# Narrower dst one-hots, group by group, in a sorted gather–transform–scatter on one core

## The chip, the core and the metric

The kernel runs on one core of a Trainium2 chip. The metric is the time of one execution on the device in microseconds (us), and the median of several executions counts. In this text PE is TensorE, DVE VectorE, ACT ScalarE, POOL GpSimd and SP SyncE.

## What is computed

There are 4096 nodes with 256 features and 262144 edges. Every edge takes the features of its source node, multiplies them by `w_msg`, and adds the result to the row of its destination node; every node also gets its own features times `w_self`.

```
self_out = nodes @ w_self
msg = nodes[edges_src] @ w_msg
np.add.at(agg, edges_dst, msg)
return self_out + agg
```

The inputs are drawn with a fixed seed, so the edges are the same in every execution.

## The kernel before

The kernel never gathers rows. It counts how many edges lead from a source to a destination and multiplies the counts by Y = nodes @ w_msg.

**Sort (first 153 us).** Each edge becomes one number, its key. In the key stand the segment of 373 destinations, the block of 128 sources, the destination inside the segment and the source inside the block. A sorting network of min and max operations on DVE (lines 854 to 1080) puts the keys nearly in order; PE and ACT turn columns and, beside that, compute Y. SP queues the loads of the edges, then the store of the nodes in bf16 and 64 transposing loads of XT (lines 211 to 280). POOL fills constants and then issues the loads of the weights and nodes (lines 218 to 272).

**Count (153 to 418 us).** The sorted edges form 2048 chunks of 128. A chunk's smallest key gives its base, and its edges lie within W = 96 steps of destination above it. For groups of chunks (`sizes`, line 466: 37 groups, most of them 64 chunks) DVE writes one-hots (`onehots`, line 471): `e_oh`, 128 columns for the source, and `d_oh`, W columns for the destination. They come in pieces of 16 columns, so a group of 64 chunks has eight pieces of `e_oh` and six of `d_oh`, each of 1024 elements a partition; two buffers of each exist, so DVE is at most two groups ahead. For every chunk PE loads `e_oh` as weights and streams the W columns of `d_oh` (`count_mm`, lines 534 and 741) into one of six PSUM banks at a place that a register gives (`poff`). A bank holds the counts of one run: 374 columns of one segment and source block, and W more as spill into the next run. There are 352 runs. The first chunks of a run meet empty columns, so `clear` (line 547) first streams zeros over two strips of GAP = 84 columns; GAP is also the largest step between two bases that is allowed.

**Apply.** When a run is complete, ACT casts its bank to SBUF (`evac`, line 556, 470 columns), and PE multiplies it with Y in three matmuls of 256 columns (`apply_run`, line 617). The spill of the run before is added either by a fourth matmul (line 623, for early runs and the last four) or by DVE (`merge`, line 577), which joins consecutive runs into one add when all of them are there. After each of 11 segments ACT copies the output rows (line 634) and POOL adds them to the output in DRAM.

**Order.** The code is written out in order of issue; nothing is rescheduled. While PE works on one group, DVE writes the one-hots of the next in four pieces of code, and the merges stand between them (line 719). The second half of the chunks gets its last sort steps during the count phase (`late_work`, line 423). `next_bases`, `misplaced` and `total` (lines 659 to 687) test that every chunk kept to its limits; if one did not, a slow general path follows (line 774).

Of the kernel before, what the change touches and what calls it, by code (L numbers as in the profile page):

```python
# [9 lines left out]
P = 128  # L10
# [110 lines left out]
def kernel(  # L121
# [230 lines left out]
    def bases(h, own):  # L352
        z = slice(h * GP, (h + 1) * GP)
        sort.note(
            nc.vector.tensor_reduce(out=k16[:, z], in_=_view3(own, P), axis=AX.X, op=ALU.min), SIZE
        )
        sort.note(muladd(k16i[:, z], k16[:, z], 1, D6 * P), GP)
        sort.note(tss(out=g7[:, z], in_=k16i[:, z], scalar=-P, op=ALU.bitwise_and), GP)
        sort.note(muladd(g7f[:, z], g7[:, z], 1 if h else -1, TOP - D6 * P if h else D6 * P), GP)

# [104 lines left out]

    sizes = [8, 24, 32, 40, 48] + [NC] * 12 + [56, 48] + [NC] * 15 + [32, 16, 16]
    assert sum(sizes) == NCOL and sum(sizes[:19]) == SIZE
    late = list(late_work())
    due = sum(cost for cost, _ in late)

    def onehots(c, n, res):
        if c in split_at:
            split_vals(c, split_at[c])
# [13 lines left out]
        for w, (nm, wid, row) in enumerate((("e", P, jrow), ("d", W, drow))):  # L487
            o = ohp.tile([P, NC // 2, wid, 2], BF16, name=nm + "_oh", tag=nm, bufs=2)
            if n <= 16:
                shp = [P, n // 2, wid, 2]  # L490
                tt(
                    out=o[:, 0:n // 2], in0=pair[:, g, w].unsqueeze(2).to_broadcast(shp),
                    in1=row[:].unsqueeze(1).to_broadcast(shp), op=ALU.is_equal,
                )
            else:
                for j in range(0, wid, NW):
# [50 lines left out]
    def clear(r):  # L547
        b = (r % RING) * BW
        after = [evac_of[r - RING]] if r >= RING else []
        zone = bass.AP(  # L550
            tensor=ring.tensor, offset=ring[:, b:b + 1].offset,
            ap=[list(ring[:].ap[0]), [SW + W - GAP, 2], [1, GAP]],
        )
        count_mm(zone, zer[:, 0, :], zer[:, 1:3, 0:GAP], True, after)

    def evac(r):
        at = ats[r % NAT]
        b = (r % RING) * BW
        ins = nc.scalar.copy(out=at[:, 0:SW + W], in_=ring[:, b:b + SW + W]).ins  # L559
        tc.declare_no_dep(  # L560
            ins, group="count", keep=[last_mm[0]], reason="disjoint banks by static schedule"
        )
        tc.add_manual_dep(ins, last_mm[0].name, DEP, reason="run complete")
        tc.add_to_no_dep_group("evac", ins)
        evac_of[r] = ins
        at_of[r] = at
# [10 lines left out]
    def merge(upto):  # L577

        upto = min(upto, NRUN - TAIL - 1)
        while merged[0] < upto:  # L580
# [20 lines left out]
    def apply_run(r):  # L601
# [14 lines left out]
        for t in range(NT):  # L616
# [54 lines left out]
    def misplaced():  # L671
# [19 lines left out]
    if True:  # L691
# [11 lines left out]
        for c in range(NCOL):  # L703
# [26 lines left out]
            if c % NREG == 0:  # L730
# [380 lines left out]
```

## Time and profile before

| what | us |
|---|---|
| median of 3 executions (426.31 to 427.47) | 426.39 |
| the profiled execution | 428.29 |
| span of its trace | 426.5 |

A trace lists for each engine when an instruction began and how long it took. Matmuls overlap in the pipeline, so their cost is the distance from one start to the next, not the duration that is printed; the same holds, to a smaller degree, on DVE. A line of the timeline joins instructions of one kind that follow each other ("x5"), with the start of the first and the time to the end of the last.

### The profile page before, as it was taken

The numbers are of one execution on the slowest core, as the hardware profiler recorded it, in microseconds if no ns is written. First come the engines' busy times: TensorE is split into PE (matmuls) and PEld (weight loads), VectorE is DVE, ScalarE is ACT, GpSimd is POOL, SyncE is SP. The second block draws the span as 40 slices with busy tenths as digits, with TensorE's granted clock in tenths as the row PEclk, the third lists the DMA queues.
The fourth block names the chain that finished last, engine by engine and source line by source line (L and its number), as shares of the span: only waits on it lengthen the run. The fifth ranks groups of instructions, "written<-read, shape, count | busy, mean of one in ns | idle before, by whom it ended". The sixth has DMA issues, their size and how long they took to land.

```text
span 426.5 us, 10578 instructions
## 1 busy us (share of the span) xinstructions
PE 339.9 (80%) x4085; PEld 288.7 (68%) x4094; DVE 383.8 (90%) x892; ACT 254.1 (60%) x515; POOL 39.1 (9%) x59
## 2 busy tenths in 40 slices
PE   0004950878787689999989899899999999999994
PEld 0001530455555357999988898798989988989993
DVE  7999999999999989999999979679999999999750
ACT  3200220155468047877777779697877877877771
POOL 5300000000000000002010030111101020102010
PEclk9999995899999899999999999699999999999999
DMA  8796111111119200003021030221203030303031
GB/s 314 141 159 197 28 24 27 25 27 25 25 32 308 79 0 2 2 2 39 0 26 16 2 37 5 55 33 15 27 2 38 6 33 4 38 2 37 4 37 38
DMA packets 31600, 20.38 MB, mean 48 GB/s; under 512 B 13244, under 2 KB 30397, under 8 KB 31549
## 3 DMA queue, kind: packets, MB, share of 16 engines
q0 software_dynamic: 8976, 6.18, 12.5%
q1 hardware_dynamic: 21876, 11.53, 9.1%
q10 hardware_dynamic: 697, 1.98, 1.2%
q8 instruction: 33, 0.54, 0.5%
q14 instruction: 18, 0.15, 0.1%
HBM read 8.92 MB, written 10.76 MB: 46 GB/s over the span
## 4 chain that ended last, share of the span: by engine, by line
PE 50%; DVE 38%; ACT 6%; issue 3%; DMA 2%; SPq 0%; DVEq 0%; ACTq 0%
PE out_ps L617 20%; PE ring L535 20%; DVE XA L866 18%; DVE XS L866 6%; DVE e_oh L511 5%; DVE d_oh L511 4%; PE out_ps L623 3%; PE tp_sw L992 3%; ACT atr L559 2%; PE warm L886 2%; DMA d<-in_edges_dst_dram 2%; DVE off L478 2%; DVE atr L589 1%; PE out_ps L745 1%; ACT XA L996 1%
## 5 line engine op out<-in xcount | busy, mean ns | idle before, releaser
L559 ACT CAST atr<-ring 128x470 bf16<-128x470 f32 x352 | 180.0, 556 | 58.4 <-PE ring L535 53.2
L617 PE MATMUL out_ps<-Y,atr 128*128 128x256 bf16 x1056 | 169.0, 274 | 3.3 <-ACT o_sb L635 2.7
L535 PE MATMUL ring<-d_oh,e_oh 128*128 128x96 bf16 x2048 | 154.5, 207 | 3.0 <-DVE d_oh L511 1.9
L535 PEld LDWEIGHTS <-e_oh 128*128 128x128 bf16 x2048 | 136.5, 98 | 9.0 <-issue 2.3
L617 PEld LDWEIGHTS <-atr 128*128 128x128 bf16 x1056 | 95.9, 98 | 9.9 <-issue 2.8
L866 DVE TENSOR_TENSOR XA<-XA 128x512 f32<-128x512 f32 (+32 forms) x142 | 92.8, 702 | 3.7 <-ACT XA L996 2.0
L511 DVE TENSOR_SCALAR e_oh<-off 128x1024 bf16<-128x1024 int16 (+5 forms) x254 | 87.1, 404 | 9.2 <-PE ring L535 6.2
L535 PE MATMUL ring<-zer 128*128 128x168 bf16 x352 | 82.9, 235 | 3.9 <-ACT atr L559 3.8
L886 PE MATMUL warm<-zw 128*128 128x512 bf16 x97 | 32.0, 442 | 56.1 <-DVE XA L866 51.2
L511 DVE TENSOR_SCALAR d_oh<-off 128x1024 bf16<-128x1024 int16 (+5 forms) x204 | 69.1, 402 | 0.0
L758 POOL DMA_DIRECT2D out_dram<-o_sb x30 | 30.2, 1007 | 363.1 <-ACT atr L559 363.1
L996 ACT COPY XA<-tp_sw 128x512 f32<-128x512 f32 x24 | 14.2, 592 | 77.8 <-PE tp_sw L992 77.8
L886 PEld LDWEIGHTS <-zw 128*128 128x128 bf16 x105 | 10.5, 107 | 73.8 <-issue 45.7
L478 DVE TENSOR_TENSOR off<-pair,rows 128x2048 int16<-128x2048 int16 (+5 forms) x34 | 38.8, 1140 | 1.2
L535 PEld LDWEIGHTS <-zer 128*128 128x128 bf16 x352 | 34.1, 97 | 8.3 <-ACT atr L559 5.6
L623 PE MATMUL out_ps<-Y,atr 128*96 128x256 bf16 x118 | 32.1, 272 | 0.0
L589 DVE TENSOR_TENSOR atr<-atr 128x288 bf16<-128x288 bf16 (+3 forms) x84 | 23.0, 293 | 8.9 <-ACT atr L559 8.7
L992 PE MATMUL tp_sw<-XA,id 128*128 128x128 f32 x192 | 24.3, 278 | 6.1 <-DVE XA L866 6.0
L992 PEld LDWEIGHTS tp_sw<-XA,id 128*128 128x128 f32 x192 | 22.4, 190 | 9.5 <-DVE XA L866 3.6
L287 PE MATMUL y_ps<-wcat,XT 128*128 128x256 bf16 x128 | 20.8, 270 | 7.4 <-ACT Y L291 3.3
L866 DVE TENSOR_TENSOR XS<-XS 128x512 f32<-128x512 f32 (+16 forms) x40 | 24.1, 653 | 0.5
L866 DVE TENSOR_TENSOR XR<-XR 128x1004 f32<-128x1004 f32 (+13 forms) x28 | 23.1, 868 | 0.2
(107 smaller groups left out, 175.9 us busy)
## 6 DMA issues: line engine op xcount, KB each, us to landing
out_dram<-o_sb POOLq DMA_DIRECT2D x20, 128.0 KB, 3.4
nodes_bf<-in_nodes_dram POOLq DMA_DIRECT2D x1, 2048.0 KB, 16.7
nodes_bf_dram<-nodes_bf SPq DMA_DIRECT2D x1, 2048.0 KB, 8.7
out_dram<-nodes_bf SPq DMA_DIRECT2D x4, 512.0 KB, 5.1
out_dram<-XA SPq DMA_DIRECT2D x4, 512.0 KB, 2.9
out_dram<-o_sb POOLq DMA_DIRECT2D x10, 117.0 KB, 3.1
s<-in_edges_src_dram ACTq DMA_DIRECT2D x2, 512.0 KB, 5.1
d<-in_edges_dst_dram SPq DMA_DIRECT2D x2, 512.0 KB, 6.0
```

Source lines behind the costliest of these rows:

```text
L287: nc.tensor.matmul(out=y_ps[:], lhsT=XT[:, k, t * P:(t + 1) * P], rhs=wcat[:, k0 + k, :], start=(k == 0), stop=(k == 1),)
L478: tt(out=v[:, 0:n // 2].rearrange("p g w (k i) -> p (g w) k i", i=2), in0=pair[:, g].rearrange("p g w i -> p (g w) i").unsqueeze(2).to_bro ...
L511: ins = tss(out=o[:, 0:n // 2, j:j + m].rearrange("p g k i -> p g (k i)"), in_=v[:, 0:n // 2, w, 0:2 * m], scalar=float((0 if w else ON_AC ...
L535: mm = nc.tensor.matmul(out=ap, lhsT=lhsT, rhs=rhs, start=start, stop=True, skip_group_check=True,).ins
L559: ins = nc.scalar.copy(out=at[:, 0:SW + W], in_=ring[:, b:b + SW + W]).ins
L589: tt(out=atr[:, j:j + n, 0:W], in0=atr[:, j:j + n, 0:W], in1=atr[:, i:i + n, SW:SW + W], op=ALU.add,)
L617: nc.tensor.matmul(out=out_ps[:, t, :], lhsT=at[:, t * P:(t + 1) * P], rhs=Y[:, b, :], start=(b == 0 and not last and t % 2 == 0), stop=(b ...
L623: nc.tensor.matmul(out=out_ps[0:W, 0, :], lhsT=spill[:, SW:SW + W], rhs=Y[:, b, :], start=False, stop=False, skip_group_check=True,)
L758: nc.gpsimd.dma_start(out=dst, in_=src, accum_op=ALU.add).ins,
L866: self.nc.vector.tensor_tensor(out=out, in0=in0, in1=in1, op=op),
L886: self.nc.tensor.matmul(out=w[:], lhsT=self.zw[:, 0:P], rhs=self.zw[:], start=True, stop=True).ins
L992: self.nc.tensor.matmul(out=tp[:, g * P:(g + 1) * P], lhsT=self.turned(rots[8 * h + 4 * t + g]), rhs=sel(x)[:, 4 * t + g], start=True, sto ...
```

## The change

Each group of chunks now has, in a table, its own width of `d_oh` and its own largest step (`GROUPS`: chunks, width, step). The widths are 80 to 95, on average 90.3 per chunk. Everything that followed W or GAP follows the table: the last of the six pieces of `d_oh` is cut to width − 80 columns, the count matmul streams only the width, the clear streams two strips of step plus the difference of the widths that a run meets, the cast takes 374 columns plus the widest spill, and a merge takes only runs of equal spill together. The destination values are shifted so that a narrower one-hot uses the last columns of the same row of constants. The shift and the step test need a value per chunk, so POOL writes a small table with 111 memsets, and two more DMAs of SP bring it to all partitions (`by_q`).

```diff
+GROUPS = [
+    (8, 80, 73), (24, 89, 73), (32, 90, 77), (40, 92, 77), (48, 92, 79), (64, 91, 82),
+    (64, 90, 81), (64, 89, 81), (64, 88, 78), (64, 93, 82), (64, 92, 79), (64, 88, 82),
+    (64, 94, 79), (64, 92, 79), (64, 90, 78), (64, 93, 77), (64, 92, 80), (56, 90, 83),
+    (48, 85, 77), (64, 88, 75), (64, 90, 80), (64, 95, 78), (64, 91, 80), (64, 87, 80),
+    (64, 89, 79), (64, 87, 83), (64, 87, 80), (64, 90, 79), (64, 91, 81), (64, 90, 77),
+    (64, 91, 79), (64, 90, 81), (64, 89, 82), (64, 95, 82), (32, 94, 79), (16, 91, 81),
+    (16, 88, 75),
+]
...
+    c = 0
+    for n, wid, gap in GROUPS:
+        z = slice(c // GP, (c + n) // GP)
+        shift = (W - wid) * P
+        for i, v in enumerate((gap, D6 * P + shift, TOP - D6 * P - shift)):
+            nc.gpsimd.memset(brow_c[:, i, z], float(v))
+        c += n
+    nc.sync.dma_start(tab_d[:, :], brow_c[:].rearrange("o t m -> o (t m)"))
+    nc.sync.dma_start(
+        by_q[:], tab_d.rearrange("o (t h q) -> q (o t) h", t=3, h=PARTS)
+    )
...
+    def about(r):
+        c0, c1 = max(0, clear_at(r) - 1), min(NCOL - 1, evac_at(r) + 1)
+        z = GROUPS[group_of[c0]:group_of[c1] + 1]
+        return max(w for _, w, _ in z), min(w for _, w, _ in z), max(g for _, _, g in z)
...
-                        in_=v[:, 0:n // 2, w, 0:2 * m], scalar=float((0 if w else ON_ACT) - j),
+                        in_=v[:, 0:n // 2, w, 0:2 * m], scalar=float((-j0 if w else ON_ACT) - j),
...
-        count_mm(zone, zer[:, 0, :], zer[:, 1:3, 0:GAP], True, after)
+        count_mm(zone, zer[:, 0, :], zer[:, 1:3, 0:n], True, after)
...
-        ins = nc.scalar.copy(out=at[:, 0:SW + W], in_=ring[:, b:b + SW + W]).ins
+        n = SW + spill_of(r)
+        ins = nc.scalar.copy(out=at[:, 0:n], in_=ring[:, b:b + n]).ins
...
+            m = spill_of(d - 1)
+            while (
+                n < min(upto - d + 1, NAT - i, NAT - j) and not by_pe(d + n)
+                and spill_of(d + n - 1) == m
+            ):
                 n += 1
...
-        stt(out=bad[:], in0=v[:], scalar=float(GAP), in1=bad[:], op0=ALU.is_gt, op1=ALU.add)
+        tt(
+            out=v[:].rearrange("p (h k) -> p h k", h=PARTS),
+            in0=v[:].rearrange("p (h k) -> p h k", h=PARTS),
+            in1=by_q[:, 0, :].unsqueeze(2).to_broadcast([P, PARTS, GP]), op=ALU.is_gt,
+        )
+        tt(out=bad[:], in0=bad[:], in1=v[:], op=ALU.add)
...
             count_mm(
-                ring[:, bass.ds(off, W)], e[:, ci // 2, :, ci % 2], d[:, ci // 2, :, ci % 2], False
+                ring[:, bass.ds(off, wid)], e[:, ci // 2, :, ci % 2], d[:, ci // 2, 0:wid, ci % 2],
+                False,
             )
```

On DVE, the second half of the count phase: the one-hots of chunks 1408 to 1471, from the middle of `e_oh` on. `atr` is the row of casted runs that a merge adds to; 32x32 is 32 pairs of chunks by 16 columns of two. Before:

```order
L511 TENSOR_SCALAR e_oh<-off 128x32x32 x5
L589 TENSOR_TENSOR atr<-atr 128x3x96
L511 TENSOR_SCALAR e_oh<-off 128x32x32 x2
L511 TENSOR_SCALAR d_oh<-off 128x32x32 x3
L589 TENSOR_TENSOR atr<-atr 128x4x96
L511 TENSOR_SCALAR d_oh<-off 128x32x32 x3
```

The same place after the change, with a width of 87:

```order
L552 TENSOR_SCALAR e_oh<-off 128x32x32 x5
L637 TENSOR_TENSOR atr<-atr 128x2x87
L637 TENSOR_TENSOR atr<-atr 128x89
L552 TENSOR_SCALAR e_oh<-off 128x32x32 x2
L552 TENSOR_SCALAR d_oh<-off 128x32x32 x3
L637 TENSOR_TENSOR atr<-atr 128x4x89
L552 TENSOR_SCALAR d_oh<-off 128x32x32 x2
L552 TENSOR_SCALAR d_oh<-off 128x32x14
```

The last piece shrinks to rows of 14 elements, and the merge of three runs becomes one of two and one of one, because the spills are 87 and 89 wide.

On POOL, at the program's start, where the constants end and the DMAs of the weights and nodes begin. Before:

```order
L264 COPY rows<-jrow 128x32
L265 COPY rows<-drow 128x32
L268 DMA wcat<-in_w_self_dram 128x2x256
L270 DMA wcat<-in_w_msg_dram 128x2x256
L272 DMA nodes_bf<-in_nodes_dram 128x32x256
```

After, from the 61st of the 111 memsets on:

```order
L283 MEMSET brow_c 1x8 x45
L283 MEMSET brow_c 1x4 x3
L283 MEMSET brow_c 1x2 x6
L290 DMA wcat<-in_w_self_dram 128x2x256
L292 DMA wcat<-in_w_msg_dram 128x2x256
L294 DMA nodes_bf<-in_nodes_dram 128x32x256
```

All memsets stand ahead of the three DMAs. On SP, two DMAs are put ahead of the store of the nodes and the 64 transposes. After the change:

```order
L222 DMA s_4_143<-in_edges_src_dram 128x224
L277 DMA kd<-ones_sent 1x1
L285 DMA tab_d<-brow_c 1x768
L286 DMA by_q<-tab_d 128x6x1
L295 DMA nodes_bf_dram<-nodes_bf 128x32x256
L298 DMA_TRANSPOSE XT<-nodes_bf_dram 128x128 x64
```

## Rows read from the trace of the kernel before

**Rows 1.** Page: busy time by engine, granted clock in 40 slices

```profile
PE 339.9 (80%) x4085; PEld 288.7 (68%) x4094; DVE 383.8 (90%) x892; ACT 254.1 (60%) x515; POOL 39.1 (9%) x59
...
PEclk9999995899999899999999999699999999999999
```

**Rows 2.** Windows of the count phase: length, busy us by engine, PEclk, DMA

```profile
153.70:256.00 102.30, 97.45 (x1333) 89.22 (x1335) 96.54 (x236) 77.20 (x143) 8.79 (x9) 1.00 0.11 13
256.00:277.00 21.00, 18.48 (x229) 16.07 (x227) 16.29 (x52) 16.22 (x35) 1.17 (x2) 0.84 0.14 30
277.00:297.00 20.00, 19.30 (x281) 17.67 (x278) 17.60 (x52) 17.68 (x35) 3.53 (x3) 1.00 0.16 20
297.00:338.00 41.00, 40.40 (x606) 38.01 (x604) 39.66 (x108) 33.41 (x68) 4.72 (x5) 1.00 0.18 21
338.00:384.00 46.00, 44.58 (x658) 41.46 (x657) 44.85 (x129) 35.56 (x72) 7.09 (x7) 1.00 0.17 19
384.00:418.00 34.00, 33.84 (x489) 31.63 (x486) 24.04 (x68) 25.34 (x50) 4.89 (x6) 1.00 0.21 25
```

**Rows 3.** Timeline of PE: start, us to the end of the last, what

```profile
310.23 0.23 PE L535 MATMUL ring<-zer 128*128 128x168 bf16 x1
310.30 0.38 PE L535 MATMUL ring<-d_oh,e_oh 128*128 128x96 bf16 x5
310.52 0.81 PE L617 MATMUL out_ps<-Y,atr 128*128 128x256 bf16 x6
```

**Rows 4.** Timeline of DVE over one group of 64 chunks

```profile
310.60 1.23 DVE L478 TENSOR_TENSOR off<-pair,rows 128x2048 int16<-128x2048 int16 x1
...
312.55 1.76 DVE L511 TENSOR_SCALAR e_oh<-off 128x1024 bf16<-128x1024 int16 x5
314.22 0.35 DVE L589 TENSOR_TENSOR atr<-atr 128x384 bf16<-128x384 bf16 x1
314.49 0.76 DVE L511 TENSOR_SCALAR e_oh<-off 128x1024 bf16<-128x1024 int16 x2
...
316.17 0.45 DVE L589 TENSOR_TENSOR atr<-atr 128x96 bf16<-128x96 bf16 x3
316.52 1.10 DVE L511 TENSOR_SCALAR d_oh<-off 128x1024 bf16<-128x1024 int16 x3
317.66 1.23 DVE L478 TENSOR_TENSOR off<-pair,rows 128x2048 int16<-128x2048 int16 x1
```

**Rows 5.** Groups by shape on DVE: busy us, mean ns, idle before

```profile
L511 DVE TENSOR_SCALAR d_oh<-off 128x1024 bf16<-128x1024 int16 x162 | 58.3, 423 | 0.0
...
L511 DVE TENSOR_SCALAR d_oh<-off 128x512 bf16<-128x512 int16 x12 | 2.7, 289 | 0.0
...
L461 DVE TENSOR_SCALAR pair<-vals_r 128x512 int16<-128x512 int16 x2 | 1.2, 603 | 0.0
```

**Rows 6.** Where one-hots end and PE begins on them: PE's timeline

```profile
296.77 0.21 PE L535 MATMUL ring<-d_oh,e_oh 128*128 128x96 bf16 x1 [0.67 <-DVE d_oh L511]
...
355.71 0.25 PE L535 MATMUL ring<-d_oh,e_oh 128*128 128x96 bf16 x2
```

**Rows 7.** Chain of waits in order of time: start, us, what

```profile
269.25 1.44 PE out_ps L617 x6
...
278.62 0.66 PE out_ps L617 x6
...
354.59 1.02 DVE d_oh L511 x3
```

**Rows 8.** Timeline of POOL at the start

```profile
3.50 0.09 POOL L257 MEMSET top<- 128x1 f32 x1
3.54 0.09 POOL L258 MEMSET limit<- 128x1 f32 x1
...
14.37 0.88 POOL L268 DMA_DIRECT2D wcat<-in_w_self_dram  x1 [7.87 <-ACT XS L232]
```

**Rows 9.** Timeline of PE at the end of the sort

```profile
141.77 4.44 PE L886 MATMUL warm<-zw 128*128 128x512 bf16 x11 [3.44 <-DVE XS L866]
```

More of the change, by code (lines that the diff above doesn't have):

```diff
@@ L147 @@
     kd = dram.tile([1, NCOL + 1], FP32, name="kd")
+    tab_d = dram.tile([1, 3 * NCOL // (NCOL // PARTS // P)], FP32, name="tab_d")
     order = tc.manual_schedule()
@@ L247 @@
     ones_sent = const.tile([1, 1], FP32, name="ones_sent")
+    brow_c = const.tile([1, 3, NCOL // GP], FP32, name="brow_c")
+    by_q = const.tile([P, 3, PARTS], FP32, name="by_q")
     jrow = const.tile([P, P, 2], I16, name="jrow")
@@ L358, in bases @@
         sort.note(tss(out=g7[:, z], in_=k16i[:, z], scalar=-P, op=ALU.bitwise_and), GP)
-        sort.note(muladd(g7f[:, z], g7[:, z], 1 if h else -1, TOP - D6 * P if h else D6 * P), GP)
+        sort.note(
+            stt(
+                out=g7f[:, z], in0=g7[:, z], scalar=1.0 if h else -1.0,
+                in1=by_q[:, 1 + h, h:h + 1].to_broadcast([P, GP]), op0=ALU.mult, op1=ALU.add,
+            ), GP
+        )
     def offsets(h):
@@ L464, with spill_of @@
     split_at = {0: 32, 32: 152, 152: 600, 600: SIZE, SIZE: SIZE + 512, SIZE + 512: NCOL}
-    sizes = [8, 24, 32, 40, 48] + [NC] * 12 + [56, 48] + [NC] * 15 + [32, 16, 16]
-    assert sum(sizes) == NCOL and sum(sizes[:19]) == SIZE
+    sizes = [n for n, _, _ in GROUPS]
+    assert sum(sizes) == NCOL
     late = list(late_work())
     due = sum(cost for cost, _ in late)
+    group_of = [g for g, n in enumerate(sizes) for _ in range(n)]
+    def about(r):
+        c0, c1 = max(0, clear_at(r) - 1), min(NCOL - 1, evac_at(r) + 1)
+        z = GROUPS[group_of[c0]:group_of[c1] + 1]
+        return max(w for _, w, _ in z), min(w for _, w, _ in z), max(g for _, _, g in z)
+    def spill_of(r):
+        return about(r)[0]
     def onehots(c, n, res):
+        width = GROUPS[group_of[c]][1]
         if c in split_at:
@@ L488, in onehots @@
             o = ohp.tile([P, NC // 2, wid, 2], BF16, name=nm + "_oh", tag=nm, bufs=2)
+            j0 = (0, W - width)[w]
+            wid -= j0
             if n <= 16:
@@ L491, in onehots @@
                 tt(
-                    out=o[:, 0:n // 2], in0=pair[:, g, w].unsqueeze(2).to_broadcast(shp),
-                    in1=row[:].unsqueeze(1).to_broadcast(shp), op=ALU.is_equal,
+                    out=o[:, 0:n // 2, 0:wid],
+                    in0=pair[:, g, w].unsqueeze(2).to_broadcast(shp),
+                    in1=row[:, j0:].unsqueeze(1).to_broadcast(shp), op=ALU.is_equal,
                 )
@@ L549, in clear @@
         after = [evac_of[r - RING]] if r >= RING else []
+        most, least, gap = about(r)
+        n = gap + most - least
         zone = bass.AP(
             tensor=ring.tensor, offset=ring[:, b:b + 1].offset,
-            ap=[list(ring[:].ap[0]), [SW + W - GAP, 2], [1, GAP]],
+            ap=[list(ring[:].ap[0]), [SW + most - n, 2], [1, n]],
         )
-        count_mm(zone, zer[:, 0, :], zer[:, 1:3, 0:GAP], True, after)
+        count_mm(zone, zer[:, 0, :], zer[:, 1:3, 0:n], True, after)
     def evac(r):
@@ L586, in merge @@
             n = 1
-            while n < min(upto - d + 1, NAT - i, NAT - j) and not by_pe(d + n):
+            m = spill_of(d - 1)
[3 more added lines that the diff above has]
+            ):
                 n += 1
             tt(
-                out=atr[:, j:j + n, 0:W], in0=atr[:, j:j + n, 0:W],
-                in1=atr[:, i:i + n, SW:SW + W], op=ALU.add,
+                out=atr[:, j:j + n, 0:m], in0=atr[:, j:j + n, 0:m],
+                in1=atr[:, i:i + n, SW:SW + m], op=ALU.add,
             )
@@ L622, in apply_run @@
             if t == 0 and r > 0 and by_pe(r):
+                m = spill_of(r - 1)
                 nc.tensor.matmul(
-                    out=out_ps[0:W, 0, :], lhsT=spill[:, SW:SW + W], rhs=Y[:, b, :],
+                    out=out_ps[0:m, 0, :], lhsT=spill[:, SW:SW + m], rhs=Y[:, b, :],
                     start=False, stop=False, skip_group_check=True,
@@ L675, in misplaced @@
         tt(out=v[:], in0=gn[:], in1=gi[:], op=ALU.subtract)
-        stt(out=bad[:], in0=v[:], scalar=float(GAP), in1=bad[:], op0=ALU.is_gt, op1=ALU.add)
+        tt(
+            out=v[:].rearrange("p (h k) -> p h k", h=PARTS),
+            in0=v[:].rearrange("p (h k) -> p h k", h=PARTS),
+            in1=by_q[:, 0, :].unsqueeze(2).to_broadcast([P, PARTS, GP]), op=ALU.is_gt,
+        )
+        tt(out=bad[:], in0=bad[:], in1=v[:], op=ALU.add)
         stt(
-            out=bad[0:1, 0:1], in0=gi[0:1, 0:1], scalar=float(GAP - 1 - SW * OFF),
+            out=bad[0:1, 0:1], in0=gi[0:1, 0:1], scalar=float(GROUPS[0][2] - 1 - SW * OFF),
             in1=bad[0:1, 0:1], op0=ALU.is_gt, op1=ALU.add,
```

2 lines of the change are left out of this document (1 added, 1 removed).

## Prediction

> **What bounds the kernel now.** Read the page's busy times and clock first [rows 1]. DVE is busy for 90% of the span and PE for 80%, but these are averages over a sort that DVE alone drives and a count phase in which PE has no idle time to speak of. So the second view is the windows of the count phase [rows 2]: PE is busy 97.45 of 102.30 us, then 40.40 of 41.00 and 33.84 of 34.00, and DVE is nearly as full up to 384 us (96.54, 39.66, 44.85 of 46.00) and slack after it (24.04). Both must become faster for the phase to become faster.
>
> The third view tells what a matmul costs on PE [rows 3]. Five count matmuls of 96 columns start at 310.30 and the next instruction at 310.52: 44 ns each. A clear of 168 columns takes 70 ns (310.23 to 310.30), and six matmuls of 256 columns 0.66 us, 110 ns each [rows 7]. [...] A group of 64 chunks with 11 runs needs 64 x 44 + 11 x 70 + 33 x 109 ns = 7.18 us of PE when no fourth matmul is issued.
>
> The fourth view is DVE over one such group [rows 4]: from the subtraction at 310.60 to the next at 317.66 there is 7.06 us of uninterrupted work. The two differ by 0.1 us, so I also ask how early one-hots are ready when PE wants them [rows 6]. At 296.77 PE had idled 0.67 us for DVE. At 355.71 PE begins a group whose last piece ended at 354.59 + 1.02 = 355.61 [rows 7]: 0.10 us of lead, none to spare. Between these two points DVE is the second limit.
>
> **Part 1, columns on PE.** The count matmuls stream the sum over the groups of chunks x width, 185,032 columns where 2048 x 96 = 196,608 stood: 11,576 fewer. The 352 clears stream 56,800 where 59,136 stood (two strips of step + widest − narrowest spill around the run): 2,336 fewer. Together 13,912 columns x 0.417 ns = 5.8 us, if time follows columns.
>
> The doubt is whether it does for short matmuls. A line through the rows of 168 and 256 columns puts 96 at 70 − 72 x 0.42 = 40 ns, and the row shows 44, so something fixed is in it. No row has a count matmul of another width. The bounds are 0 (the pair of weight load and matmul never goes below 44 ns) and 2.4 ns for each matmul at the mean width of 90.3. I take the full 0.417 ns a column, because the two nearest rows, 70 ns for 168 columns and 110 for 256, follow their columns (70.0 and 106.7 ns) closely, and each of those matmuls has a weight load too.
>
> [...]
>
> **Part 2, DVE.** The last of the six pieces of `d_oh` shrinks. Pieces of 1024 and 512 elements last 423 and 289 ns [rows 5], so an element costs 0.262 ns. A group of n chunks loses (96 − width) x n elements: 11,240 over all groups in pieces, 2.9 us. The merges become 102 where 84 stood, because runs of unequal spill are no longer joined, with 21,116 elements where 22,368 stood. A merge of 384 elements takes 314.49 − 314.22 = 0.27 us and one of 96 takes 0.35/3 = 0.117 us [rows 4], so an element costs 0.53 ns and an instruction 0.066 us: 18 x 0.066 − 1252 x 0.00053 = +0.5 us. The step test has one more small instruction, about 0.2 us. DVE loses 2.2 us net.
>
> This takes for granted that rows of 14, 18 or 26 elements, and merges of odd width (60 of the 102 have one, 12,336 elements), run at the rate of the even ones. No row shows an odd width. The bounds are nothing and the rate of the access that DVE does slowly: the split of `vals_r`, 512 elements in 603 ns against 289 for a compact piece of 512 [rows 5], 0.31 us more, or 0.6 ns an element. I take nothing, because each row is still contiguous and the number of rows even.
>
> [...]
>
> **Part 3, what is hidden.** ACT's cast loses 1 to 15 of 470 columns; ACT is not the limit (33.41 of 41 us [rows 2]), so this counts for nothing. The 111 memsets stand on POOL before the loads of weights and nodes. POOL is idle for 7.87 us before the first of these, until 14.37 [rows 8], and small memsets start 0.04 us apart (3.50, 3.54): 4.4 us, covered. At their printed 0.09 us each they would take 10 us and delay the loads by 2.1 us. SP carries two more DMAs ahead of the store of the nodes; SP has nothing else to do until the nodes land, which is after both. A delay would reach the last transposes and with them the projections on PE, behind which PE stands idle for 3.44 us until 141.77 [rows 9]. Cost 0; it would show from 3.4 us of delay on. The table's first use comes at the end of the sort, long after it has landed, and replaces an instruction on DVE by one of equal size.
>
> **The sum.** By stretches, since the two engines change places. Groups are counted from 0, and each saving of PE is its columns x 0.417 ns.
> - Groups 0 to 15 (to 276 us): 5,460 columns, 2.28 us. PE sets the pace here, except for groups 0 to 2, for which DVE has had no time to get ahead; there DVE's 0.16 us counts instead of 0.27. Gain 2.17.
> - Groups 16 to 18: at the end PE waits for DVE (296.77). DVE's pieces lose 56 x 6 + 48 x 11 + 64 x 8 = 1,376 elements, 0.36 us. Gain 0.36, not the 0.52 of PE.
> - Groups 19 to 26 (to 355.7): PE could gain 4,072 columns, 1.70 us. DVE loses 64 x 52 elements = 0.87 us, has 0.2 more for merges and 0.2 for the test: 0.48 net. With the lead of 0.10 the gain is 0.6.
> - Groups 27 to 36: 3,130 columns, 1.30 us. Beyond 384 DVE is slack [rows 2]. Gain 1.3.
>
> Together 4.4 us: the profiled execution goes from 428.29 to 423.9. It lies 1.9 us above the median of 426.39, and the same difference taken from that gives **422.0 us**.
>
> **Rivals.**
> 1. *A pair of weight load and count matmul keeps its 44 ns.* For: the 4 ns over the line. Against: 44 is so near to 96 columns. Only the clears gain on PE, 2,336 x 0.417 = 1.0 us, with some 0.1 from DVE: 425.3.
> 2. *Odd merges run at half rate.* For: nothing in the rows excludes it. DVE gets 6.5 us more, nearly all after 277 us, where merges are. Groups 0 to 15 keep their 2.17. In groups 19 to 26 DVE is 2.5 us slower instead of 0.5 faster, and with no lead PE waits for all of it; after that PE's 1.3 meets a loss of the same size. About 426.5, no change.
> 3. *Ragged rows throw the last piece of `d_oh` out of its fast rate*, and that is the slower side. For: shape alone doubles an instruction's time in the split of `vals_r` [rows 5]. Against: its rows are of 2 elements, these of 10 and more. The 34 last pieces have 20,888 elements; at 0.6 ns more each DVE gets 12.7 us, 0.4 per group. It decides once a group costs DVE more than PE's new 7.0 us: groups 17 to 19 lose 0.5, groups 20 to 27 2.5, later ones about 0.5, against 2.0 gained before: 427.9. If the odd merges go the same way, 432. I price it at 430.
> 4. *PE's clock.* One stretch runs at the lower level: six matmuls take 1.44 us at 269.25 and 0.66 at 278.62 [rows 7], after waits for ACT. The window of 21 us around it has a mean clock of 0.84 [rows 2], so it loses 21 x 0.16 = 3.4 us. With PE's waits moved, it may vanish (418.6) or come twice (425.4).
> 5. *The table does not fit the edges*, and the general path runs. The draw is fixed, and worked out from it the widest chunk of every group equals the group's width, and the largest step its bound. 1%; it would be milliseconds.
>
> **How the numbers follow.** About 0.3%, 1.3 us, is what a measurement here can tell from no change; faster means under 425.1. Forecast 0.62 (419.9 to 424.5), first rival 0.13, second 0.10, third 0.10, fourth 0.04, fifth 0.01. Faster: the forecast, nearly half of the first rival, half of the fourth, 0.68. Same: the rest of the first, the second, 0.20. Slower: the third and the fifth with a tail of the second, 0.12. The range from 420.0 to 427.0 leaves out the slow half of the third and little else.
>
> **What would show it.** The timeline of PE has count matmuls of 90 columns 41 to 42 ns apart and of 80 columns 37; 44 ns at all widths is the first rival. The merges by shape: four runs of 91 in about 0.35 us; 0.55 means half rate. The last pieces of `d_oh` in 0.26 to 0.35 us; 0.8 is the third. PE's waits for `d_oh` grow between 320 and 356 us, and from there PE has none. POOL ends its memsets by 11 us, and the sort ends when it did, with PE's first count matmul within 0.3 us of 153.9. I am wrong if PE's pairs become shorter and the phase does not: then a wait of ACT or DVE has taken their place.

## The result, and the profile after

The changed kernel took 422.63 us in the median (421.70, 422.11, 423.15 and 425.16), the kernel before 426.35 us beside it (426.21 to 427.47): ratio 0.9888, with an interval from 0.9849 to 0.9928. The forecast was 422.0 us, range 420.0 to 427.0. Timed again (run e5 below), the changed kernel took 423.31 us against 426.75, ratio 0.9904 [0.9868, 0.9940]. The ratio is not the quotient of the medians: the medians alone give 3.7 and 3.4 us, the ratios 4.8 and 4.1. The gain is about 4 us.

The profiled execution of the changed kernel is the slowest of its four (425.16 us, span 423.0), and that of the kernel before lies above its median too (428.29, span 426.5). So I read it beside the profile of e5, whose span is 421.0 us.

The page of the changed kernel: busy time, and the granted clock in 40 slices, as in [rows 1].

```profile
PE 335.4 (79%) x4085; PEld 282.9 (67%) x4094; DVE 381.3 (90%) x911; ACT 252.3 (60%) x515; POOL 45.6 (11%) x170
...
PEclk9999995899999898999999999999999999999999
```

PE lost 4.5 us of busy time, DVE 2.5; POOL gained 6.5, of which its 111 memsets are 3.8. The 6 that stood at 267 to 277 us before is gone; an 8 at 159 to 169 us is new.

The windows of the count phase, columns as in [rows 2], and one of six us within the first:

```profile
160.00:166.00 6.00, 5.71 (x48) 3.25 (x48) 5.54 (x18) 3.05 (x6) 0.00 (x0) 0.72 0.01 3
...
153.70:256.00 102.30, 96.74 (x1323) 87.29 (x1323) 94.66 (x233) 76.31 (x142) 11.75 (x9) 0.98 0.11 13
256.00:277.00 21.00, 18.46 (x268) 16.66 (x265) 18.81 (x63) 18.45 (x40) 1.84 (x2) 1.00 0.16 32
...
297.00:338.00 41.00, 40.36 (x618) 37.92 (x616) 39.74 (x123) 33.64 (x70) 6.13 (x6) 1.00 0.16 18
338.00:384.00 46.00, 44.02 (x653) 40.28 (x652) 43.95 (x128) 34.88 (x71) 7.41 (x7) 1.00 0.19 21
384.00:418.00 34.00, 33.18 (x465) 30.44 (x463) 21.35 (x66) 23.65 (x48) 3.52 (x5) 1.00 0.18 22
```

PE is as full as before. From 297 to 338 us it puts 618 matmuls where 606 stood, in the same busy time: matmuls became shorter, and idle time did not grow much. The timeline of PE shows it, here with the rows that answer to [rows 3] and [rows 6]:

```profile
153.94 0.31 PE L576 MATMUL ring<-d_oh,e_oh 128*128 128x80 bf16 x4
154.09 0.23 PE L576 MATMUL ring<-zer 128*128 128x164 bf16 x1
...
160.11 0.20 PE L576 MATMUL ring<-d_oh,e_oh 128*128 128x90 bf16 x1 [1.18 <-DVE d_oh L552]
...
160.22 0.42 PE L576 MATMUL ring<-d_oh,e_oh 128*128 128x90 bf16 x6
160.47 0.23 PE L576 MATMUL ring<-zer 128*128 128x154 bf16 x1
...
162.80 3.31 PE L801 MATMUL out_ps<-zw 128*128 128x512 bf16 x8
...
294.49 0.20 PE L576 MATMUL ring<-d_oh,e_oh 128*128 128x88 bf16 x1 [0.61 <-DVE d_oh L552]
...
352.22 0.25 PE L576 MATMUL ring<-d_oh,e_oh 128*128 128x90 bf16 x2 [0.24 <-DVE d_oh L552]
```

Four matmuls of 80 columns start within 0.15 us, 37 ns each; six of 90 within 0.25 us, 42 ns each. The wait for DVE that stood at 296.77 is there still (0.61 us after 0.67), and at 352.22 there is one where a lead of 0.10 had been.

By stretches, from the start of the first count matmul of each group on the timelines (us; the third column is a run with the table set back to one width, e1 below):

| groups | before | uniform table | changed | changed again | forecast gain |
|---|---|---|---|---|---|
| 0 to 14 | 109.48 | 109.48 | 110.37 | 108.08 | 2.17 with group 15 |
| 15 | 13.09 | 11.65 | 10.29 | 11.93 | |
| 16 to 18 | 20.30 | 20.30 | 19.89 | 19.87 | 0.36 |
| 19 to 26 | 58.94 | 59.11 | 57.73 | 57.76 | 0.60 |
| 27 to the end | 70.80 | 70.95 | 70.82 | 69.60 | 1.30 |

Group 15 is a matter of the clock: these windows from 262 to 277 us give the granted clock in the third column from the right. The kernel before, the changed kernel again, and e8 (the same work but for rounded widths):

```profile
262.00:277.00 15.00, 12.48 (x140) 10.55 (x138) 10.39 (x34) 11.04 (x26) 1.17 (x2) 0.77 0.19 41
```

```profile
262.00:277.00 15.00, 12.47 (x160) 10.74 (x157) 11.59 (x35) 12.05 (x27) 2.36 (x3) 0.89 0.29 52
```

```profile
262.00:277.00 15.00, 12.46 (x186) 11.23 (x184) 12.68 (x40) 13.58 (x30) 3.35 (x3) 1.00 0.31 55
```

At a clock of 1.00 group 15 takes 10.3 us (e8 10.31), at 0.89 11.9, at 0.77 13.1. In the first profile of the changed kernel a stretch at the lower level lies at 160 to 166 us instead (0.72 in its window above, 0.50 from 163 to 165 us): eight fillers of 512 columns (matmuls that only keep PE at work while it waits) take 3.31 us at 162.80 on the timeline above. The kernel before needs 1.89 us for the same eight, so groups 0 to 14 lose some 1.6 us; a pause of 0.50 us after chunk 399 comes on top.

```profile
162.81 1.89 PE L745 MATMUL out_ps<-zw 128*128 128x512 bf16 x8
```

Where these stretches do not differ (changed again against the uniform table, both with 0.89 in group 15) the gains are 1.40, nothing in group 15, 0.43, 1.35 and 1.35 us, 4.5 in all. Of the last, only 0.33 us lie ahead of the end of PE's last matmul (65.01 us from the start of group 27 in e1, 64.68 in e5); 1.0 us lies behind it, where the last rows are stored. From PE's last matmul to the end of the span it takes 5.9 to 6.1 us in the kernel before, e1 and e2, 4.9 to 5.0 us with the table's own widths (5.3 and 5.4 in e7 and e10). The times of the last stores, first e1, then e5:

```profile
DMA to landing us min/median/max: 2.6/3.0/3.4
```

```profile
DMA to landing us min/median/max: 2.3/2.3/2.4
```

Why they land sooner is not shown. In the first three kernels two packets of another queue, q14 "instruction", run during these stores, in the changed kernel one.

### The profile page after: what moved, and what is told of

The parts are those of the page before. It is cut to its first block, busy times and chain, and to the rows that moved or that the text cites. A ratio compares the mean times of both kernels' runs of the same rounds, so it can differ in the third digit from the quotient of the medians.

```text
span 423.0 us, 10713 instructions
## 1 busy us (share of the span) xinstructions
PE 335.4 (79%) x4085; PEld 282.9 (67%) x4094; DVE 381.3 (90%) x911; ACT 252.3 (60%) x515; POOL 45.6 (11%) x170
## 4 chain that ended last, share of the span: by engine, by line
PE 50%; DVE 38%; ACT 5%; issue 3%; DMA 2%; SPq 0%; DVEq 0%; ACTq 0%
PE out_ps L665 20%; PE ring L576 19%; DVE XA L922 18%; DVE XS L922 6%; DVE e_oh L552 5%; DVE d_oh L552 3%; PE out_ps L672 3%; PE tp_sw L1048 3%; PE warm L942 2%; DMA d<-in_edges_dst_dram 2%; DVE off L516 2%; ACT atr L603 2%; DVE atr L637 1%; PE out_ps L801 1%; ACT XA L1052 1%
## 5 line engine op out<-in xcount | busy, mean ns | idle before, releaser
L603 ACT CAST atr<-ring 128x464 bf16<-128x464 f32 (+8 forms) x352 | 178.2, 554 | 58.0 <-PE ring L576 53.5
L576 PE MATMUL ring<-d_oh,e_oh 128*128 128x90 bf16 (+10 forms) x2048 | 149.4, 204 | 3.7 <-DVE d_oh L552 2.0
L576 PEld LDWEIGHTS <-e_oh 128*128 128x128 bf16 x2048 | 132.4, 97 | 10.2 <-issue 3.9
L665 PEld LDWEIGHTS <-atr 128*128 128x128 bf16 x1056 | 94.7, 97 | 10.9 <-issue 4.4
L576 PE MATMUL ring<-zer 128*128 128x164 bf16 (+11 forms) x352 | 82.2, 233 | 4.1 <-ACT atr L603 4.0
L814 POOL DMA_DIRECT2D out_dram<-o_sb x30 | 32.9, 1098 | 357.9 <-ACT atr L603 357.9
L552 DVE TENSOR_SCALAR d_oh<-off 128x1024 bf16<-128x1024 int16 (+5 forms) x204 | 66.1, 386 | 0.0
L672 PE MATMUL out_ps<-Y,atr 128*92 128x256 bf16 (+6 forms) x118 | 32.1, 272 | 0.0
L637 DVE TENSOR_TENSOR atr<-atr 128x360 bf16<-128x360 bf16 (+24 forms) x102 | 24.0, 264 | 7.4 <-ACT atr L603 7.4
```

What stands on the lines that cost most here:

```text
L552: ins = tss(out=o[:, 0:n // 2, j:j + m].rearrange("p g k i -> p g (k i)"), in_=v[:, 0:n // 2, w, 0:2 * m], scalar=float((-j0 if w else ON_ ...
L576: mm = nc.tensor.matmul(out=ap, lhsT=lhsT, rhs=rhs, start=start, stop=True, skip_group_check=True,).ins
L603: ins = nc.scalar.copy(out=at[:, 0:n], in_=ring[:, b:b + n]).ins
L637: tt(out=atr[:, j:j + n, 0:m], in0=atr[:, j:j + n, 0:m], in1=atr[:, i:i + n, SW:SW + m], op=ALU.add,)
L665: nc.tensor.matmul(out=out_ps[:, t, :], lhsT=at[:, t * P:(t + 1) * P], rhs=Y[:, b, :], start=(b == 0 and not last and t % 2 == 0), stop=(b ...
L672: nc.tensor.matmul(out=out_ps[0:m, 0, :], lhsT=spill[:, SW:SW + m], rhs=Y[:, b, :], start=False, stop=False, skip_group_check=True,)
```

## The experiments

Each run was timed beside the kernel before on its own chip, so ratios are compared, not times.

### e1: the table alone

```
+GROUPS = [(n, 96, 84) for n, _, _ in GROUPS]
```

> The changed code with every row of its table set back to width 96 and step bound 84: table, memsets, broadcast DMAs and the extra test are there, no column is saved. Theory (the gain is columns; the table is hidden): as the kernel before, 426.4 us, 425.5 to 427.5. Rival (the table or its DMAs cost time on the chain ahead of the first chunk): 427.5 or more, with the first count matmul later than 154.2 us.

426.77 us against 426.49, ratio 1.0003 [0.9979, 1.0027]. The first count matmul starts at 153.87 us. The table, its two DMAs and the added test cost nothing that can be measured; the theory holds. In the changed kernel the memsets are one row of POOL's timeline, done by 10.3 us, and the load that they could have delayed starts 0.12 us later than in [rows 8]:

```profile
6.46 3.84 POOL L283 MEMSET brow_c<- 1x1 f32 x111
14.49 0.89 POOL L290 DMA_DIRECT2D wcat<-in_w_self_dram  x1 [4.19 <-ACT XS L241]
```

### e2: one width of 95 for all

```
+GROUPS = [(n, 95, 83) for n, _, _ in GROUPS]
```

> One width for all groups, the largest of the table: 95 columns and bound 83. It saves one column of 2,048 count matmuls (0.85 us) and 2 of each clear (0.07 us), and one sixteenth of DVE's last piece. Theory (time follows columns): 425.5 us, 424.5 to 426.5. Rival (the widths of single groups are not needed, what counts is to leave 96): 422.6 us as the changed kernel.

427.23 us against 426.49, ratio 1.0023 [1.0003, 1.0043]. Both theories missed: one column less saves nothing. PE's timeline of this kernel has five matmuls of 95 columns within 0.22 us, the 44 ns of 96:

```profile
310.49 0.38 PE L577 MATMUL ring<-d_oh,e_oh 128*128 128x95 bf16 x5
310.71 0.71 PE L666 MATMUL out_ps<-Y,atr 128*128 128x256 bf16 x5
```

In the changed kernel's trace the median from start to start within bursts is 37 ns at 80 columns, 40 at 85 to 88, 42 at 89 to 92, 43 to 44 at 93, 44 at 94 and 95: steps of four columns, each some 1.7 ns by the forecast's estimate of 0.417 ns a column. e8 asks whether that is so.

### e3 and e4: each half of the change alone

e3 leaves DVE's last piece at full width:

```
-            wid -= j0
             if n <= 16:
+                wid -= j0
```

> The changed kernel with DVE's six d_oh pieces at their full 16 columns: TensorE streams the narrow one-hots, DVE builds 96 columns as before (the surplus ones are not read). Theory: the 5.8 us of columns carry the gain and DVE's 2.9 us matter only where TensorE waits for it, groups 19 to 26 and the first three groups: 423.3 us, 422.5 to 424.5, with more idle of TensorE for d_oh between 290 and 356 us. Rival (DVE's last piece carries half the gain or more): 425 us or more.

424.16 us, ratio 0.9942 [0.9919, 0.9964]: the theory's median within 0.9 us. On its timeline the waits for DVE between 290 and 356 us grew, from 0.61 and 0.24 us to 0.73 and 0.59:

```profile
292.57 0.20 PE L576 MATMUL ring<-d_oh,e_oh 128*128 128x88 bf16 x1 [0.73 <-DVE d_oh L552]
...
351.11 0.25 PE L576 MATMUL ring<-d_oh,e_oh 128*128 128x90 bf16 x2 [0.59 <-DVE d_oh L552]
```

Groups 19 to 26 take 58.54 us instead of 57.76 (e5), and groups 16 to 18 take 20.23, as with the uniform table (20.30), instead of 19.87. e4 streams 96 columns again, as two overlapping halves of 48:

```
-        n = gap + most - least
+        n, most = 84, W
...
-                ring[:, bass.ds(off, wid)], e[:, ci // 2, :, ci % 2], d[:, ci // 2, 0:wid, ci % 2],
+                ring[:, bass.ds(off, W)].rearrange("p (t j) -> p t j", t=2),
+                e[:, ci // 2, :, ci % 2],
+                bass.AP(
+                    tensor=d.tensor, offset=d[:, ci // 2, 0:1, ci % 2].offset,
+                    ap=[list(d[:].ap[0]), [2 * (wid - W // 2), 2], [2, W // 2]],
+                ),
```

> The other half: DVE builds only the narrow one-hots and merges narrow spills, TensorE streams 96 columns again (two overlapping halves of the narrow ones, so the counts are not those of the reference; the clears are 2 x 84 again). Theory: only the waits for DVE go, some 0.7 us of those seen near 296 and 355 us, less if the wait at the head is not DVE's width: 425.6 us, 424.7 to 426.6. Rival (DVE carries half the gain or more): 424.5 us or less.

427.38 us, ratio 1.0016 [0.9997, 1.0034]: no gain, where I had expected 0.8 us; both theories missed. But e4 does not tell what DVE's half is worth alone, because its two overlapping halves cost PE time of their own. The mean distance from start to start of its count matmuls is 44.9 ns, against 44.0 in e1 (distances of 60 ns and more, which hold waits, left out). Over 2048 matmuls that is 1.9 us, and the clears add 0.3: about as much as the 1.8 us by which e4 is later than 425.6. PE's waits for DVE fell from 2.2 us in e1 to 1.4, which is the 0.8 us expected, though a slower PE waits less in any case. Once PE is faster, DVE's half is worth some 0.4 us in groups 16 to 18 and 0.8 us in groups 19 to 26 (e3 against e5).

### e8 and e11: what a pair of weight load and matmul costs

e8 rounds widths up to multiples of 4:

```
+GROUPS = [(n, -(-w // 4) * 4, g) for n, w, g in GROUPS]
```

> Every width of the table rounded up to a multiple of 4 (80 to 96), step bounds as they are: 3,040 columns more are streamed by the count matmuls. Theory (start to start of a pair goes in steps of 4 columns: 40 ns at 85 to 88, 42 at 89 to 92, 44 at 93 to 96): the changed kernel's time, within 0.5 us, since no pair takes longer; DVE has fewer merges and larger last pieces. Rival (columns count one by one, the trace's steps are its clock ticks): 1.3 us later than the changed kernel.

(The number in it should be 2,904 columns, 187,936 less 185,032; by the rival that is 1.2 us.) 422.69 us, ratio 0.9907 [0.9874, 0.9940], beside 0.9904 for the changed kernel in the same comparison. The profiled spans, 420.5 against 421.0 us, say less: e5's holds the lower clock in group 15, and outside that group e8 is 1.2 us later, 0.8 of it in group 23, where a pause of 0.63 us stands after chunk 1319. Its timeline has six matmuls of 92 columns in 0.25 us, 42 ns each, as at 90:

```profile
170.72 0.42 PE L577 MATMUL ring<-d_oh,e_oh 128*128 128x92 bf16 x6
170.97 0.23 PE L577 MATMUL ring<-zer 128*128 128x158 bf16 x1
```

The theory holds: from 85 to 96 columns PE pays in fours (40, 42 and 44 ns). The distances, not the totals, decide it, since the intervals of the two ratios are wider than 1.2 us. Nor do the steps come from whole nanoseconds in the trace, as the rival has it: the means too are level within a step, 42.5, 42.6, 42.3 and 42.4 ns at 89 to 92 columns in e5, 44.0, 44.0 and 43.9 at 93 to 95, and the mean over all count matmuls is 42.3 ns in e8, 42.2 in e5. e11 goes far below:

```
+        n = SW + most
+        count_mm(ring[:, b:b + n], zw[:, 0:P], zw[:, 0:n], True, after)
...
-                ring[:, bass.ds(off, wid)], e[:, ci // 2, :, ci % 2], d[:, ci // 2, 0:wid, ci % 2],
+                ring[:, bass.ds(off, 48)], e[:, ci // 2, :, ci % 2], d[:, ci // 2, 0:48, ci % 2],
```

> One look at the pace of a pair: the count matmuls stream only the first 48 columns of each one-hot (the others' counts are left out), and each clear writes the whole run, so the span says nothing. Theory (columns set the pace, as from 96 down to 80): 48 x 0.417 + 3.3 = 23 ns start to start within a burst. Rival (the weight load sets a floor below 80 columns): 30 to 36 ns.

Six matmuls of 48 columns start within 0.15 us, 25 ns each, the median of 1,495. 23 ns were expected and 30 or more for a floor below 80 columns; so columns set the pace well below 80. Whether the 25 ns are themselves a floor, one width does not tell.

```profile
300.56 0.31 PE L576 MATMUL ring<-d_oh,e_oh 128*128 128x48 bf16 x6
300.71 0.36 PE L576 MATMUL ring<-zw 128*128 128x464 bf16 x1
```

### e5, e6, e7: the clock, and a surprise

e5 is the changed kernel, unaltered.

> The changed kernel itself, unaltered, timed beside the next three on one chip. Theory (its profile showed a half-clock stretch at 160 to 166 us that only part of its executions have): median 422.5 us, 421.5 to 423.5, and a profile without that stretch has a span near 420.5 us. Rival (the stretch belongs to the change, as TensorE now waits longer for d_oh at 158.5 us): it is in this profile again.

423.31 us, ratio 0.9904 [0.9868, 0.9940], profiled span 421.0 us. The wait at 158.5 us is there (1.15 us) and no stretch of lower clock follows it (granted clock 1.00 from 153.7 to 168 us), so that stretch does not belong to the change, nor does the wait alone bring it. e6 covers the wait:

```
-FILL = {8: 10, 32: 3, 64: 8}
+FILL = {8: 10, 32: 8, 64: 8}
```

> The changed kernel with 8 filler matmuls of 512 columns before chunk 32 in place of 3: they take some 1.1 of the 1.18 us in which TensorE waited there for d_oh. Theory (the wait at 158.5 us brings the half-clock stretch at 160 to 166 us in part of the executions): no such stretch, chunk 56 near 164.5 us, median 0.3 to 1.0 us below the changed kernel's. Rival (the stretch has nothing to do with that wait): same median within 0.3 us; or, if the fillers run over the wait, 0.1 to 0.3 us later.

424.96 us, ratio 0.9947 [0.9919, 0.9974]: the wait is gone and nothing was gained (groups 0 to 14 take 108.07 us, 108.08 in e5); the median is 1.6 us above e5's, so both theories missed. The intervals of the two ratios overlap; in the profiles 1.2 us stand in groups 19 to the end (58.05 and 70.53 us, against 57.76 and 69.60). e7 adds the fillers ahead of the waits for ACT:

```
+MID = {640: 10, 809: 8, 824: 9}
...
+            for _ in range(MID.get(c + 1, 0)):
+                b = (nev % RING) * BW
+                count_mm(ring[:, b:b + 256], zw[:, 0:P], zw[:, 0:256], False)
```

> As the run before, and also zero matmuls of 256 columns before three waits for ScalarE: 10 at 242.6 us (1.37 us idle), 8 at 265.8 (1.06 us), 9 at 268.7 (1.22 us). They add zero to the counts. Theory (the half-clock stretch at 266 to 276 us comes from these waits, in part of the executions): that stretch is in none, the times lie closer together, median 0.3 to 1.0 us below the run before. Rival (ScalarE ends these waits and no stretch hangs on them): same median within 0.3 us.

425.72 us, ratio 0.9970 [0.9944, 0.9996]: no gain again, and a median 0.8 us above e6's, against both theories. Up to group 24 its profile does what was intended: group 15 takes 10.29 us at a clock of 1.00. Six of the twelve profiles without these fillers have 0.77 or 0.89 there, neither of the two with them (this and e10); that points to the waits and does not show it. Then 4.1 us are lost in groups 24 and 25, most of it in one pause of PE for which the profile names no releaser ("issue"):

```profile
342.73 0.29 PE L577 MATMUL ring<-d_oh,e_oh 128*128 128x87 bf16 x3 [2.52 <-issue]
```

Such pauses stand in every profile. On e5's timeline (the first three lines are waits for ACT, of which e9 speaks):

```profile
214.68 0.27 PE L665 MATMUL out_ps<-Y,atr 128*128 128x256 bf16 x1 [0.96 <-ACT o_sb L684]
...
241.63 0.24 PE L576 MATMUL ring<-zer 128*128 128x158 bf16 x1 [1.37 <-ACT atr L603]
...
267.66 1.40 PE L665 MATMUL out_ps<-Y,atr 128*128 128x256 bf16 x6 [1.23 <-ACT o_sb L684]
...
343.43 0.21 PE L576 MATMUL ring<-d_oh,e_oh 128*128 128x87 bf16 x1 [0.32 <-issue]
...
369.39 0.82 PE L665 MATMUL out_ps<-Y,atr 128*128 128x256 bf16 x6 [0.82 <-issue]
...
378.63 0.20 PE L576 MATMUL ring<-d_oh,e_oh 128*128 128x91 bf16 x1 [0.26 <-issue]
```

These three follow chunks 1466, 1687 and 1759, and so they do in the kernel before, e1, e3, e8 and the first profile of the changed kernel, wherever they are long enough to be seen; some profiles have one elsewhere too (after 399 in e2, after 1319 in e8). In e6, whose row of PE instructions is ten longer, they follow 1463, 1536, 1830 and 1902. A pause of 0.25 us after chunk 815 is of another kind: e6 and e7 have it at the same chunk.

### e10 and e12: where the pauses come from

e10 is e7 without its stores:

```
-                for t, n in ((0, P), (1, P), (2, m)):
+                for t, n in ():
```

> The kernel of e7 (fillers at the head and at three waits) without the 30 stores that POOL issues during the count phase, so the rows of all segments but the last stay unwritten. It asks where the pauses of TensorE come from that no wait explains: 6.3 us in e7's profile, 3.8 to 5.2 us in those of the changed kernel, 2.3 to 3.7 us in those at 95 and 96 columns. Theory (the stores' transfers hold up what TensorE fetches): they fall under 2 us, the median to 421 us or less. Rival (the stores have no part in it): pauses of 3 us or more, median 424.5 us or more.

424.73 us, ratio 0.9937 [0.9911, 0.9962], with a pause of 2.28 us after chunk 1447, the same place as in e7. The theory fell: the stores do not make the pauses. e12 puts the instructions back in their places:

```
-FILL = {8: 10, 32: 3, 64: 8}
+FILL = {8: 10, 32: 8, 64: 3}
```

> e6 was 1.6 us slower than the changed kernel although its five extra fillers lay inside a wait. TensorE's pauses without a wait stood at the same chunks in every kernel with the same row of TensorE instructions (after chunks 1466, 1687 and 1759, in the kernel before too), and at 1463, 1683 and 1830 in e6, whose row is ten instructions longer. Here the five fillers are taken away again before chunk 64 (3 in place of 8 there), so from chunk 64 on each instruction has the place that it has in the changed kernel. Theory (the pauses hang on an instruction's place in the program): pauses at 1466, 1687 and 1759 again, median 423.3 us, 422.3 to 424.0. Rival (the fillers at the head cost the time in another way): pauses elsewhere, median 424.5 us or more.

422.25 us, ratio 0.9900 [0.9876, 0.9924], and the pauses are back after 1466, 1687 and 1759:

```profile
343.54 0.21 PE L576 MATMUL ring<-d_oh,e_oh 128*128 128x87 bf16 x1 [0.59 <-issue]
...
369.62 0.82 PE L665 MATMUL out_ps<-Y,atr 128*128 128x256 bf16 x6 [0.90 <-issue]
...
378.85 0.20 PE L576 MATMUL ring<-d_oh,e_oh 128*128 128x91 bf16 x1 [0.27 <-issue]
```

The theory holds (the median even lies 0.05 us below its range): a pause hangs on an instruction's place in the program, and moving the row by ten instructions cost some 1.6 us.

Two counts over all fourteen profiles tie the pauses to the place and to a DMA queue. Number PE's instructions in the order in which they start, weight loads, matmuls and its sequencer's, 8,468 in e5 (nine matmuls are missing from the traces of the kernel before and of the first changed one, and are counted in). Of the 47 pauses over 0.15 us in the count phase, those after chunk 815 left out, 46 stand at places 193 to 200 of a block of 256 instructions; the other, of 0.15 us in e2, stands at 213. And all 47 end 1.26 to 2.26 us after a packet on one DMA queue has ended, however long the packet took.

The transfers on DMA by queue (queue and kind, packets, MB, share of 16 engines) list that queue as "instruction". In e7 between 337 and 341 us, ahead of the long pause, its one packet took 5.1% of 16 x 4 us, 3.3 us; in e5 between 340 and 344 us, 1.6%, 1.0 us:

```profile
q8 instruction: 1, 0.02, 5.1%
```

```profile
q8 instruction: 1, 0.02, 1.6%
```

In e10 it is 3.2%, 2.0 us. The page of the changed kernel has for the whole span:

```profile
q8 instruction: 33, 0.54, 0.6%
```

These are 16.4 KB a packet, and 8,468 instructions of PE over 33 packets are 257 a packet, which fits a block of 256 and a place in it that does not change. That the packets bring PE's instructions is my estimate from this count and the queue's kind. The three pauses on e5's timeline come to 1.4 us (0.32, 0.82 and 0.26). Most packets are followed by no pause (29 packets and three pauses in e5's count phase), so what makes a pause, and what makes a packet take 3.3 us, is not shown.

### e9: ScalarE's waits

```
+    def on_act(c):
+        return c < ACT_END and c not in (472, 664, 856)
...
-                    if i == CUTS[1] and c < ACT_END:
+                    if i == CUTS[1] and on_act(c):
```

(and `on_act(c)` at the two other places).

> The changed kernel; for the groups that begin at chunks 472, 664 and 856 VectorE builds the 16 e_oh columns that ScalarE builds in other groups (1.15 us of ScalarE each, 0.42 us of VectorE). These three slices stand right ahead of the casts and o_sb copies for which TensorE waits at 215.5 (0.35 and 1.13 us), 242.6 (1.54 us) and 268.7 us (1.38 us), waits that all profiles so far repeat. Theory (ScalarE, not columns, ends these waits): they shrink by about 1 us each, 420.5 us, 419.5 to 421.5. Rival (VectorE has no room there: it is busy 7.1 of 8 us): new waits for d_oh of 0.4 us each, 422.0 us or more.

419.60 us, ratio 0.9823 [0.9786, 0.9860]: faster than both kernels, and within the theory's range. PE's timeline has the waits at 0.60, 0.56 and 0.18 us where e5 has 0.96, 1.37 and 1.23:

```profile
214.57 0.27 PE L668 MATMUL out_ps<-Y,atr 128*128 128x256 bf16 x1 [0.60 <-ACT o_sb L687]
...
240.42 0.24 PE L579 MATMUL ring<-zer 128*128 128x158 bf16 x1 [0.56 <-ACT atr L606]
...
265.43 0.81 PE L668 MATMUL out_ps<-Y,atr 128*128 128x256 bf16 x6 [0.18 <-ACT o_sb L687]
```

Groups 9 to 14 became 1.8 us shorter. Group 15 takes 9.3 us against 10.3 in the profiles at full clock; the other 1.6 against e5 is e5's clock. VectorE had the room: groups 16 to 26 take the same time as in e5 to 0.02 us.

## Why the prediction was right, point by point

**What bounds the phase.** PE and DVE in turn, as said: e3 shows that DVE's half adds 0.4 us in groups 16 to 18 and 0.8 us in groups 19 to 26 on top of PE's. What it is worth alone is not shown (e4). In group 15 neither bounds it, but ACT (a wait of 1.23 us at 267.66 us in e5).

**Columns on PE.** The doubt was settled for the columns, but the term was too large. I had 5.8 us for the count matmuls and the clears. The mean distance from start to start (distances that hold waits left out) goes from 44.05 ns before to 42.24 in e5 for the 2048 count matmuls, 3.7 us, and from 72.1 to 70.6 for the 352 clears, 0.5 us: 4.3 us together, since columns count in fours. In fours the widths save 8,672 columns and not 11,576, which at 0.417 ns is 3.6 us. The sum's 0.417 ns a column is 70 ns over the 168 columns of one clear, an estimate: no run shows it for count matmuls, which came 44 ns apart at 96 columns, 37 at 80 and 25 at 48, or 0.44 ns a column from 96 to 80 and 0.40 from 96 to 48. (The 0.42 of the line is not that of its rows: 70 and 110 ns for 168 and 256 columns give 0.45 ns a column; the medians of 72 and 109 ns give 0.42.)

**DVE.** 2.2 us expected, 2.5 measured on the page. The pages of e1, e3 and e5 part it: 383.9, 383.9 and 381.1 us busy, so the pieces gave 2.8 us (2.9 expected), and the larger number of merges, for which I had 0.5, cost nothing that shows. Ragged and odd shapes keep their rate, as these groups by shape say (busy us, mean ns, idle before):

```profile
L552 DVE TENSOR_SCALAR d_oh<-off 128x1024 bf16<-128x1024 int16 x135 | 49.1, 420 | 0.0
...
L552 DVE TENSOR_SCALAR d_oh<-off 128x640 bf16<-128x640 int16 x11 | 3.2, 320 | 0.0
...
L637 DVE TENSOR_TENSOR atr<-atr 128x364 bf16<-128x364 bf16 x4 | 1.4, 351 | 0.0
...
L637 DVE TENSOR_TENSOR atr<-atr 128x91 bf16<-128x91 bf16 x7 | 1.2, 202 | 0.0
...
L552 DVE TENSOR_SCALAR d_oh<-off 128x448 bf16<-128x448 int16 x4 | 1.1, 271 | 0.0
```

289 + 128 x 0.262 = 323 ns is the line for 640 elements; the row has 320. Four odd runs of 91 take 351 ns, where four of 96 take 0.35 us [rows 4]. So odd widths cost no more in these merges, as the forecast took for granted.

**What is hidden.** Right: e1, the memsets' row, and the first count matmul at 153.94 after 153.90.

**The sum.** The total came out (4.4 forecast, 4.5 measured between stretches of equal clock), and that is luck in part: three of its four terms did not, and their errors cancel. Groups 0 to 15 gained 1.4, not 2.17: columns count in fours, and group 15, bound by waits for ACT, takes 10.3 us at 95 columns (e2) as at 93. Groups 16 to 18 gained 0.43 for 0.36, as forecast. Groups 19 to 26 gained 1.2 (against the kernel before) to 1.35, not 0.6. DVE does set their pace, as I had said: from the end of its pieces for group 19 to the end of those for group 27 it is hardly idle, before and in e5 (windows as in [rows 2]):

```profile
296.72:355.60 58.88, 57.72 (x860) 54.21 (x860) 56.92 (x160) 46.78 (x94) 8.22 (x9) 1.00 0.20 22
```

```profile
293.55:351.31 57.76, 56.68 (x861) 52.94 (x861) 56.13 (x167) 46.48 (x94) 8.96 (x9) 1.00 0.20 22
```

But its net saving, for which I had 0.48 us, is 1.1: 0.9 from the pieces, as forecast, 0.2 lost to merges and the test where I had 0.4, and 0.3 less idle time, for which I had nothing. Groups 27 to the end gained 1.35 for 1.30 in number only: 0.33 of it is PE's and 1.0 the sooner landing of the last stores, which I had not foreseen. In the first profile this stretch gained nothing: its PE part is 1.1 us longer than before, and pauses of 1.5 us stand in it (0.3 before).

**The rivals.** The first is out by the pace of the pairs (42 ns at 90 columns, 37 at 80), the second and third by the groups by shape (351 ns for four runs of 91; 320 and 271 ns for last pieces of 640 and 448 elements). The second's 6.5 us were an estimate, another 0.53 ns for each of 12,336 odd elements. The fourth came as well as the forecast: the stretch vanished from one profile of the changed kernel and came at another place there, and a second profile (e5) has about half of it. In full it costs 2.8 us in group 15 (13.1 against 10.3), where I had 3.4. It is no part of the change: the table at one width (e1) has it too.

## What to carry to other kernels

Here the width of the one-hots set a count matmul's cost: 43 to 44 ns at 93 to 96 columns, 42 at 89 to 92, 40 at 85 to 88, 37 at 80, 25 at 48; take each group's own width, but round it up to four. When two engines are within 2% of each other (7.18 and 7.06 us for a group, by the prediction's reading), narrow the work of both: here PE's half alone gave 0.6% (e3) and the two together 1.0 to 1.1%; DVE's half was not measured alone. Before the next cut look at the waits that all profiles repeat: three slices given from ScalarE to VectorE brought 3 us more, nearly as much as the whole change.

## What had not been expected

- PE's pauses for nothing that the profile names, 0.2 to 2.5 us each, stand at places 193 to 200 of a block of 256 instructions (one of 47 at 213) and end 1.3 to 2.3 us after a packet on q8, the queue of kind "instruction". They stay after the same chunks (1466, 1687 and 1759) in kernels with the same row of instructions, and go elsewhere (1463, 1536, 1830 and 1902) when ten instructions are put in ahead. Fillers inside a wait, which I had thought free, made the kernel some 1.6 us slower (e6) until five others were taken out (e12).
- From PE's last matmul to the end it takes 1.0 us less in every kernel with the table's own widths (0.6 in e7 and e10); no column explains it.
- Five matmuls of 95 columns take as long as five of 96 (44 ns each), and 92 as long as 90 (42 ns): from 85 to 96 columns PE's pace goes in steps of four.
- Of the same work in group 15, profiles show 13.1, 11.9 and 10.3 us at granted clocks of 0.77, 0.89 and 1.00 over the 15 us around it. One profile alone can be 3 us off at one place for no reason of the kernel.
